# Smaller matmul forms for gates, pools and context keys in a one-core hybrid block, with weight casts moved to the last attention units

## The chip, the cores and the metric

The kernel runs on one core of a Trainium2 chip. The metric is the device time of one execution in microseconds (us). The kernel before took 1061.37 us in the median of three runs (1061.03 to 1061.40).

A core has five engines that run their own instruction streams side by side and wait for one another by semaphores: TensorE (PE in the profile; its weight loads are listed as PEld), VectorE (DVE), ScalarE (ACT), GpSimd (POOL) and SyncE (SP), which here issues most DMA transfers.

## The reference: what is computed

One layer on 1024 latent tokens (a grid of 16 rows of 64) and 256 context tokens, width 1024, all in float32:

```
mod_x = silu(c) @ w_mod + b_mod              # six rows: sh1, sc1, gt1, sh2, sc2, gt2
h_x = rmsnorm(x) * (1 + sc1) + sh1           # the context's h_c likewise, from c_ctx
u, q, k, v = h_x @ w_in                      # u is 512 wide, q, k, v are 512 wide (8 heads of 64)
attn = neighbourhood_attention(q, k, v, k_c, v_c, rpb)    # 8 x 16 window and all context keys
pool: for g, w in ((0, 2), (1, 4), (2, 8), (3, 16)):      # 128 features each
    d_g = centred_mean(u_g, w) - u_g                      # along the tokens
    y_g = d_g @ pool_w[g] * pool_scale_g
mix = concat(y, attn) @ w_out
x = x + gt1 * rmsnorm(mix)
x = x + gt2 * rmsnorm(relu(rmsnorm-modulated(x) @ w1) ** 2 @ w2)
```

Three things matter here. The context's keys are `h_c @ w_in[:, k]`, and attention needs them with features on the partitions. The gates `gt1` and `gt2` are rows of 1024 values that later multiply every token. Each pool group ends in a product with a 128 x 128 matrix.

## The kernel before, in words

**Numbers in halves.** Most products run in float32r, in three passes. An operand is split into a high part (a cast on ScalarE) and a low part (the difference, on DVE): `split`, L142, and `high_low`, L151, for weights. `three`, L167, then issues high x high, high x low and low x high as three matmuls (L168 to L170) that accumulate in one PSUM bank. A product over 1024 inputs has eight k-tiles of 128, so 24 matmuls. Three small kinds of product run in plain float32 instead: the sums of the gates (L198), the context keys' transposes (L542) and the pools' products (L603).

**Stages**, in the order in which TensorE comes to them: inputs, norms and modulation; latent keys; context keys and values; latent values; the pools' projections; the queries, with both gates and the pools' products between them; attention; the output projection; and an MLP done by a Strassen scheme.

**Context keys** (L522 to L530). Per group of 128 context tokens the tokens are stationary and the weights' 512 features move: 24 matmuls of 512 columns, and ScalarE copies the bank to `kct`. Since tokens are then on the partitions, each group is turned by four float32 transposes (`pkct`, L542) in the loop of the context values, and a second ScalarE copy puts it into `kcT`.

**Gates** (`mod_gate`, L193). A row of `w_mod`'s product is summed over k-tiles on DVE (`mod_sum`, L183) into a page `acc`, which still has 128 partial sums, one to a partition. A matmul with a matrix of ones adds the partitions and leaves the row in all of them: two float32 matmuls of 512 columns. DVE multiplies each half with the gain row `gp`. One row of the result goes to DRAM and is read back later for all partitions (`gate_page`). The sums are issued piece by piece as background work: `background` (L478) advances them and runs the closing step, the gate itself, at the next call. There are four of these rows: two column forms for the MLP's shift and scale, then gate a and gate b.

**Pools.** For each of four groups, two projections (`pu{g}_{b}`, one to a half of the tokens) are copied by ScalarE (L614) into a page `u{g}`. `pooled` (L566) makes the window sums with doubling adds on DVE, using two pages `sa{g}` and `sb{g}`, repairs the edges with small operations, and leaves the difference `d`. `pool_out` (L599) multiplies it with `pwt`, two matmuls for a group (`py{g}_{b}`), and writes the scaled result as a high part (ScalarE, L605) and a low part (DVE, L606).

**Queries** (`queries`, L650). Eight projections `pq{j}_{b}`: j is a pair of heads, b a half of the tokens. The copy that scales and reverses q runs on ScalarE (L656) into a page for each two j. All of b = 0 comes first, then `pq0_1`, the pools' products, `pq1_1`; the other two stand among the first attention units.

**Attention** (loop from L837). 32 units (four pairs of heads by eight tiles of tokens), in a software pipeline of i = 0 to 35. The loads of the output weights are issued at the units in `LOADS`, and their splits, eight halves, at the units in `HALVES` (L790): `weight_split` (L805) casts on ScalarE and leaves the difference on DVE to the next unit's `low` (L797).

**What sets the order.** Inside `in_order` blocks (L103) the engines named keep the order in which the code issues. Elsewhere a scheduler decides, from dependences and buffers. Three pools matter: 33 pages of 128 x 1024 floats (`act`, L88), four raw-weight pages (`wraw`, L86) and eight pages for split weights (`whl`, L87). In PSUM there are six banks for general use and two longer-lived ones. A page or bank is taken again only when its last reader is done, and the wait for that reader stands on the engine that writes next.

Of the kernel before, what the change touches and what calls it, by code (L numbers as in the profile page):

```python
# [17 lines left out]
P = 128  # L18
D = 1024
# [60 lines left out]
def hybrid_block(ctx, tc, x, ctx_in, w_mod, b_mod, gp1, gp2, w_in, pool_w, rpb, w_out, w1, w2, vectors,  # L80
# [17 lines left out]
    def page(name, dt=F32):  # L98
        return act.tile([P, 1024], dt, tag="pg", name=name)
# [42 lines left out]
    def split(src, hi, lo):  # L142
        nc.scalar.copy(hi, src)  # L143
        nc.vector.tensor_tensor(lo, src, hi.bitcast(F32), sub)  # L144

    def load(name, src):
        raw = wraw.tile([P, 1024], F32, tag="raw", name=f"{name}w")
        nc.sync.dma_start(raw.rearrange("p (a b) -> p a b", b=src.shape[-1]), src)
        return raw
# [13 lines left out]
    def wk(w, k, lo, c, n):  # L163
        return w[k // 2][lo][:, (k % 2) * 512 + c : (k % 2) * 512 + c + n]
# [18 lines left out]
    def mod_sum(name, c, alloc, sT):  # L183
# [4 lines left out]
        for k in range(KT):  # L188
            w = load(f"wm{name}_{k}", w_mod[k * P : (k + 1) * P, c * D : (c + 1) * D])
            nc.vector.scalar_tensor_tensor(acc, w, sT[:, k : k + 1], acc, mul, add)  # L190
            yield acc

    def mod_gate(name, acc, gp, bank):  # L193
        g = load(f"gp{name}", gp.rearrange("(o d) -> o d", o=1).to_broadcast([P, D]).rearrange("p (a b) -> p a b", a=2))
        for h in range(2):
            hs = slice(h * 512, (h + 1) * 512)
            ps = bank(f"pg{name}{h}")
            nc.tensor.matmul(ps, ones, acc[:, hs], start=True, stop=True)  # L198
            nc.vector.tensor_tensor(acc[:, hs], ps, g[:, hs], mul)

    def mod_column(name, acc, bank):
        ps = bank(f"pc{name}")
# [20 lines left out]
    with tc.tile_pool(name="ps1", bufs=6, space=PSUM) as ps1, tc.tile_pool(name="tmp1", bufs=3) as tmp:  # L223

        def bank(name):
            if name[:2] == "pm" or name in ("pxt1_0", "pxt0_2", "pxt1_7", "pct2", "pct3"):
                return lasting(name)
            return ps1.tile([P, 512], F32, tag="mm", name=name)

        def once(name, shape):  # L230
            return tmp.tile(shape, F32, tag=name, name=name, bufs=1)
# [257 lines left out]
        def mod_row(name, c, gp):  # L489
            for acc in mod_sum(name, c, page, sx):  # L490
                yield

            def close():
                mod_gate(name, acc, gp, bank)
                gates[name] = dram.tile([1, D], F32, tag=f"g{name}", name=f"g{name}")
                nc.sync.dma_start(gates[name], acc[0:1, :])

            closing.append(close)

# [14 lines left out]
        def token_group(ps, w, hk):  # L514
            for k in range(KT):
                hi, lo = hk(k)
                three(ps, hi, lo, wk(w, k, 0, 0, 512), wk(w, k, 1, 0, 512), k == 0, k == KT - 1)
# [2 lines left out]
        lat_tok = lambda b, i: lambda k: (hx[b][k][:, i * P : (i + 1) * P], hx[b][k][:, 512 + i * P : 512 + (i + 1) * P])  # L520

        kcp = page("kcT")  # L522
        kct = page("kct").rearrange("p (i f) -> p i f", i=2)
        raw_v = [load(f"wv{kk}", pair(w_in, kk, 1536, 512)) for kk in range(KT // 2)]
        for i in range(2):
            ps = bank(f"pkc{i}")
            token_group(ps, wgt, ctx_tok(i))
            if i:
                wgt = [high_low(f"wv{kk}", raw_v[kk]) for kk in range(KT // 2)]
            nc.scalar.copy(kct[:, i], ps)  # L530
        startup.close()
        with tc.issue_after(last[ET.DVE]):
            background(4)
# [1 line left out]
        for i in range(2):  # L535
            ps = bank(f"pvc{i}")
            token_group(ps, wgt, ctx_tok(i))
            nc.scalar.copy(vcp[:, i * 512 : (i + 1) * 512], ps)
            background()
            pt = bank(f"pkct{i}")  # L540
            for j in range(4):
                nc.tensor.transpose(pt[:, j * P : (j + 1) * P], kct[:, i, j * P : (j + 1) * P], ident)  # L542
            nc.scalar.copy(kcp.rearrange("p (j i t) -> p i j t", j=4, i=2)[:, i],
                               pt.rearrange("p (j t) -> p j t", j=4))
        kc = kcp.rearrange("p (j t) -> p j t", j=4)

        vp = [page(f"v{i}") for i in range(4)]
        for m in range(NM):
# [10 lines left out]

        pwt = once("pwt", [P, 4, P])  # L560
        nc.sync.dma_start(pwt, pool_w.rearrange("g c d -> c g d"))
        edg = once("edg", [P, 4, 16])
        nc.sync.dma_start(edg, edge.rearrange("o (g e) -> o g e", g=4).to_broadcast([P, 4, 16]))
        dT = []
# [32 lines left out]


        def pool_out(g):  # L599
            dv = dT[g].rearrange("p (r m c) -> p m r c", r=QR, m=NM)  # L600
            for b in range(2):
                ps = bank(f"py{g}_{b}")
                nc.tensor.matmul(ps, pwt[:, g, :], dv[:, 4 * b : 4 * b + 4], start=True, stop=True)  # L603
                mp = page(f"mix1_{g}", F32R) if b else wraw.tile([P, 1024], F32R, tag="raw", name=f"mix0_{g}")
                nc.scalar.activation(mp[:, :512], ps, AF.Identity, scale=pscol[:, g : g + 1])  # L605
                nc.vector.scalar_tensor_tensor(mp[:, 512:], ps, pscol[:, g : g + 1], mp[:, :512].bitcast(F32), mul, sub)  # L606
                mix[b][g] = mp

        for g in range(4):
            up = page(f"u{g}")  # L610
            for b in range(2):
                ps = bank(f"pu{g}_{b}")
                feature_group(ps, wgt, g * P, b, range(KT))
                nc.scalar.copy(up.rearrange("p (r m c) -> p m r c", r=QR, m=NM)[:, 4 * b : 4 * b + 4],  # L614
                                   ps.rearrange("p (m r c) -> p m r c", m=4, r=QR))
            dT.append(pooled(g, up))


        tabs, msk = [], []
# [30 lines left out]
        def queries(j, b, ps, n):  # L650
            feature_group(ps, wgt, j * P, b, range(KT))
            if j % 2 == 0:
                qp[b] = page(f"q{b}_{j}")
            qT[j][b] = qp[b][:, (j % 2) * 512 : (j % 2) * 512 + 512]
            background(n)
            nc.scalar.activation(qT[j][b].rearrange("p (m t) -> p m t", t=P)[:, :, ::-1],  # L656
                                 ps.rearrange("p (m t) -> p m t", t=P), AF.Identity, scale=-(HD ** -0.5))
# [3 lines left out]
            queries(j, 0, bank(f"pq{j}_0"), (1, 2, 3, 99)[j])  # L661
        mask_page()
        tables(0)
        queries(0, 1, bank("pq0_1"), 0)
        for g in range(4):
            pool_out(g)


    with (
# [117 lines left out]

        kks = (2, 3, 0, 1)
        raw_o, wo = {}, {}
        LOADS, HALVES = (8, 10, 17, 19), (12, 13, 14, 20, 21, 22, 28, 30)  # L790
        lows = []

        def high(src, hi, lo):
# [11 lines left out]
        def weight_split(n):  # L805
            kk, cs = kks[n // 2], slice(n % 2 * 512, n % 2 * 512 + 512)
            if n % 2 == 0:
                wo[kk] = [whl.tile([P, 1024], F32R, tag="hl", name=f"wo0_{kk}{x}") for x in "hl"]
            hi, lo = wo[kk]
            high(raw_o[0, kk][:, cs], hi[:, cs], lo[:, cs])  # L810
# [22 lines left out]
            nc.vector.tensor_tensor(mp1[t][:, hs], ps, G1[:, hs], mul)  # L833

        with in_order(ET.PE, ET.Activation, ET.DVE, ET.SP):
            queries(1, 1, bank("pq1_1"), 0)
            for i in range(N + 4):  # L837
                if i < N and units[i][1] == 2 and units[i][0] < 3:
                    tables(units[i][0] + 1)
                if i in LOADS:  # L840
                    weight_load(0, kks[LOADS.index(i)])
                if i == N - 2:
                    G1 = gate_page("a")
                if i > 3:
                    weighed(i - 4)
                low()
                if i > 8 and i % 8 == 7:
                    mixed_split(i // 8 - 1, 1)
                if i > 0 and i % 8 == 0:
                    mixed_split(i // 8 - 1, 0)  # L850
                if i in HALVES:
                    weight_split(HALVES.index(i))
                if i < N:
                    scores(i)
                else:

                    if i == N:
                        po = ps_s.tile([P, 1024], F32, tag="S", name="po")[:, :512]
                    out_sums(po, wo, 0, ((0, 1), (2, 3, 4), (5, 6, 7), ())[i - N])
                if 1 < i <= N + 1:  # L860
                    turn(i - 2)
                    fifth_kept(i - 2)
                if i < N:
                    exps(i, 0)
                if 1 < i <= N + 1:
                    turn_kept(i - 2, 0, nc.scalar.copy)
                if i < N:
                    exps(i, 1)
                if 1 < i <= N + 1:
                    turn_kept(i - 2, 1, nc.vector.tensor_copy)  # L870
                if i < 2:
                    queries(2 + i, 1, bank(f"pq{2 + i}_1"), 0)
                if 0 < i <= N:
                    share(i - 1)
                if 2 < i <= N + 2:
                    values(i - 3)
            mixed_split(3, 1)
            low()
            out_kept(0, 0, po, page("jo0_0")[:, :512])
            po = bank("po1")  # L880
            out_sums(po, wo, 1, range(8))
            out_kept(0, 1, po, page("jo0_1")[:, :512])
# [497 lines left out]
```

## Time and profile before

| | |
|---|---|
| median of three runs | 1061.37 us |
| the profiled execution's own time | 1061.53 us |
| its span, first to last instruction | 1059.7 us |
| TensorE busy | 1045.5 us, 99% |
| DVE, ScalarE, GpSimd busy | 685.6, 507.5, 55.7 us |
| the two gates' matmuls | 1.72 us each |
| the eight pools' products | 6.87 us |
| the context's eight transposes | 2 x 0.44 us |

A row of a timeline or group names start (or place), busy time, engine, line, operation, the tile written and the tiles read, and the count. "idle before <-X" tells how long the engine stood before the instructions and what ended it. In the chain each row is a stretch of work that the next one waited for, or followed on the same engine. PEclk is the TensorE clock granted, 1.00 at full speed.

### The profile page before, as it was taken

The page shows a single profiled execution, that of the slowest core. Times are in us where ns is not written, and L with a number is a line of the kernel's source. Part 1 is how long each engine was busy: PE and PEld are TensorE (multiplying, and loading weights), DVE is VectorE, ACT ScalarE, POOL GpSimd, SP SyncE. Part 2 cuts the span into 40 slices and gives each one's busy share as a digit, 9 for nine tenths or more (in the row PEclk, how much of TensorE's full clock was granted, in tenths as well). Part 3 has the DMA queues.
Part 4 walks back from the last instruction along what each step waited for, and adds up shares of the span by engine and source line. Part 5 has one row for each costly group of instructions (what it writes and reads, how often), then busy time and mean ns, then how long its engine had stood idle before and what let it go on. Part 6 is the DMA issues. An engine that isn't in the chain of part 4 may idle for free.

```text
span 1059.7 us, 15246 instructions
## 1 busy us (share of the span) xinstructions
PE 1045.5 (99%) x5870; PEld 856.4 (81%) x5870; DVE 685.6 (65%) x1071; ACT 507.5 (48%) x882; POOL 55.7 (5%) x109
## 2 busy tenths in 40 slices
PE   8999999999999999999999999999999999999996
PEld 6788888867878888888888888888888888888885
DVE  5536624846998225799987666664577666557586
ACT  7563021236998123886555454554553335334441
POOL 2020000030120003200000000000000000000001
PEclk9999999999999999999999999999999999999998
DMA  9906740531111605445745345345597666556556
GB/s 342 326 21 230 240 146 0 165 107 55 35 39 57 159 1 180 147 150 182 255 169 179 130 146 182 129 159 189 212 354 263 233 238 218 198 165 206 168 191 203
DMA packets 94268, 179.37 MB, mean 169 GB/s; under 512 B 6898, under 2 KB 39154, under 8 KB 94196
## 3 DMA queue, kind: packets, MB, share of 16 engines
q1 hardware_dynamic: 76644, 144.80, 41.6%
q10 hardware_dynamic: 16272, 29.40, 7.5%
q0 software_dynamic: 1280, 4.21, 1.1%
q8 instruction: 46, 0.75, 0.3%
q14 instruction: 26, 0.21, 0.1%
HBM read 140.62 MB, written 37.76 MB: 168 GB/s over the span
## 4 chain that ended last, share of the span: by engine, by line
PE 89%; ACT 4%; DVE 3%; issue 1%; DMA 1%; POOL 1%; SPq 0%; POOLq 0%; DVEq 0%; ACTq 0%
PE pk L400 4%; PE S L697 3%; PE pyv L170 3%; PE pyz L170 3%; PE pyx L170 3%; PE pyx L168 3%; PE phz L169 3%; PE phv L169 3%; PE phv L168 3%; PE phz L168 3%; PE pyz L169 3%; PE pyv L169 3%; PE pyv L168 3%; PE pyz L168 3%; PE phv L170 3%; PE phz L170 3%
## 5 line engine op out<-in xcount | busy, mean ns | idle before, releaser
L1029 ACT ACTIVATE c<-c 128x512 f32<-128x512 f32 x48 | 30.3, 631 | 59.9 <-DVE c L1142 23.3
L720 ACT ACTIVATE sp<-sp,nm 128x640 f32<-128x640 f32 (+1 forms) x64 | 51.4, 804 | 7.8 <-DVE nm L711 7.3
L711 DVE CUSTOM_DVE_ANT_0 sp<-S,tab 128x640 f32<-128x640 f32 (+1 forms) x56 | 42.8, 802 | 16.1 <-PE S L697 9.4
L144 DVE TENSOR_TENSOR wpS<-S,wpS 128x512 fp32r<-128x512 f32 x64 | 43.6, 686 | 11.9 <-ACT wpS L143 11.9
L170 PE MATMUL phx<-thB,wpA 128*128 128x512 f32 x128 | 49.9, 390 | 0.0
L168 PE MATMUL phx<-thB,wpA 128*128 128x512 f32 x128 | 49.9, 390 | 0.0
L169 PE MATMUL phx<-tlB,wpA 128*128 128x512 f32 x128 | 49.8, 389 | 0.0
L143 ACT CAST wpS<-S 128x512 fp32r<-128x512 f32 x64 | 39.2, 616 | 18.2 <-PE phy L170 7.8
L139 POOL TENSOR_TENSOR ry<-vy,nhalf 128x1 f32<-128x1 f32 x8 | 4.4, 550 | 600.7 <-DVE vy L137 600.7
L1030 ACT ACTIVATE c<-c 128x512 f32<-128x512 f32 x48 | 30.3, 631 | 8.1 <-DVE sa L1100 7.4
L1136 DVE TENSOR_TENSOR c<-phz,u 128x512 f32<-128x512 f32 x16 | 11.0, 690 | 32.2 <-PE phz L170 32.1
L170 PEld LDWEIGHTS phx<-thB,wpA 128*128 128x128 f32 x128 | 24.0, 188 | 5.2 <-DVE wpA L144 0.2
L697 PE MATMUL S<-kT,q 64*128 64x384 f32 (+1 forms) x128 | 27.8, 495 | 0.4 <-DVE nm L711 0.4
L168 PEld LDWEIGHTS phx<-thB,wpA 128*128 128x128 f32 x128 | 24.0, 188 | 5.0
L169 PEld LDWEIGHTS phx<-tlB,wpA 128*128 128x128 f32 x128 | 24.0, 188 | 4.9
L833 DVE TENSOR_TENSOR mp<-pw,Ga 128x512 f32<-128x512 f32 x14 | 9.6, 688 | 27.5 <-ACT jo L130 27.5
L773 PE MATMUL pa<-pt,v 128*64 128x128 f32 x352 | 25.9, 279 | 1.2 <-ACT px L753 0.6
L168 PE MATMUL phy<-thT,wpS 128*128 128x512 f32 x64 | 24.9, 389 | 0.0
L169 PE MATMUL phy<-tlT,wpS 128*128 128x512 f32 x64 | 24.9, 389 | 0.0
L170 PE MATMUL phy<-thT,wpS 128*128 128x512 f32 x64 | 24.9, 389 | 0.0
L168 PE MATMUL phz<-thT,wpS 128*128 128x512 f32 x64 | 24.9, 389 | 0.0
L169 PE MATMUL phz<-tlT,wpS 128*128 128x512 f32 x64 | 24.9, 389 | 0.0
(922 smaller groups left out, 3269.4 us busy)
## 6 DMA issues: line engine op xcount, KB each, us to landing
b<-in_w SPq DMA_DIRECT2D x64, 512.0 KB, 4.6
hrS<-hdS SPq DMA_DIRECT2D x32, 512.0 KB, 5.1
hrA<-hdA SPq DMA_DIRECT2D x24, 512.0 KB, 5.5
wm<-in_w_mod SPq DMA_DIRECT2D x16, 512.0 KB, 9.7
wa_0w<-in_w SPq DMA_DIRECT2D x16, 512.0 KB, 4.9
wa_1w<-in_w SPq DMA_DIRECT2D x16, 512.0 KB, 4.0
hdA<-c ACTq DMA_DIRECT2D x32, 256.0 KB, 2.1
hdS<-sa ACTq DMA_DIRECT2D x32, 256.0 KB, 4.4
```

The source lines that it names most:

```text
L143: nc.scalar.copy(hi, src)
L144: nc.vector.tensor_tensor(lo, src, hi.bitcast(F32), sub)
L168: nc.tensor.matmul(ps, ahi, bhi, start=first, stop=False, skip_group_check=more)
L169: nc.tensor.matmul(ps, ahi, blo, start=False, stop=False, skip_group_check=more)
L170: nc.tensor.matmul(ps, alo, bhi, start=False, stop=last, skip_group_check=more)
L400: nc.tensor.matmul(pks[b][j], wk(wgt, k, low, j * P, P), r, start=(k == 0 and n == 0), stop=(k == KT - 1 and n == 2))
L697: nc.tensor.matmul(S[e][:, c0 : c0 + keys.shape[1]], q[hs, cols], keys[hs], start=True, stop=True)
L711: nc.vector.tensor_tensor_reduce(out=to, in0=s, in1=bt, scale=1.0, scalar=BIG, op0=add, op1=ALU.min, accum_out=nm)
L720: nc.scalar.activation(sp, sp, AF.Exp, bias=least[i, e], scale=-1.0, accum_out=sums[i][:, e : e + 1])
L773: nc.tensor.matmul(pa[e * HD : (e + 1) * HD, cols], v[:, f : f + HD], turns[i][:, e, c] if c < 4 else fifths[i][:, :, (e + 1) * HD : (e + ...
L1029: nc.scalar.activation(r, src, AF.Relu)
L1030: nc.scalar.activation(r, r, AF.Square)
```

## The change

Five edits.

1. Context keys are computed with features first: the weights are stationary and the 256 context tokens move. Four groups (j, 128 features each) of 24 matmuls of 256 columns; ScalarE copies each bank straight into `kcT`. The transposes, `kct` and its copies are gone.
2. A gate's row is summed in four column groups: four float32 matmuls of 256 columns, each on 32 of the array's columns, so that quarter c of the row lies on partitions 32c to 32c + 31. One DVE operation of 128 x 256 multiplies by the gain, whose quarters come by four loads; the store takes four DMAs.
3. Pools' products run in three float32r passes. Each `d` is split into high and low by halves of the tokens, in eight more pages `d{g}_{b}`; `pool_w` is split once.
4. `background()` is called after each of the pools' projections, so sums of the gates come earlier; the products from `pq0_1` to `pq1_1` keep their order on TensorE.
5. `HALVES` puts three of the eight weight splits at i = 32, 32 and 33, one at 29, and the others as before or one unit off.

In the program as built, gate a's matmuls stand behind the first projection of pool group 1 and gate b's behind the third query; before, both stood among the queries.

```diff
     def mod_gate(name, acc, gp, bank):
-        g = load(f"gp{name}", gp.rearrange("(o d) -> o d", o=1).to_broadcast([P, D]).rearrange("p (a b) -> p a b", a=2))
-        for h in range(2):
-            hs = slice(h * 512, (h + 1) * 512)
-            ps = bank(f"pg{name}{h}")
-            nc.tensor.matmul(ps, ones, acc[:, hs], start=True, stop=True)
-            nc.vector.tensor_tensor(acc[:, hs], ps, g[:, hs], mul)
+        g = wraw.tile([P, 1024], F32, tag="raw", name=f"gp{name}w")[:, :256]
+        quarters = gp.rearrange("(c o f) -> c o f", c=4, o=1)
+        for c in range(4):
+            nc.sync.dma_start(g[32 * c : 32 * c + 32, :], quarters[c].to_broadcast([32, 256]))
+        ps = bank(f"pg{name}")
+        for c in range(4):
+            nc.tensor.matmul(ps[32 * c : 32 * c + 32, :256], ones[:, :32], acc[:, c * 256 : (c + 1) * 256],
+                             start=True, stop=True)
+        nc.vector.tensor_tensor(acc[:, :256], ps[:, :256], g, mul)
...
-                nc.sync.dma_start(gates[name], acc[0:1, :])
+                for c in range(4):
+                    nc.sync.dma_start(gates[name][:, c * 256 : (c + 1) * 256], acc[32 * c : 32 * c + 1, :256])
...
         kcp = page("kcT")
-        kct = page("kct").rearrange("p (i f) -> p i f", i=2)
+        kc = kcp.rearrange("p (j t) -> p j t", j=4)
...
-        for i in range(2):
-            ps = bank(f"pkc{i}")
-            token_group(ps, wgt, ctx_tok(i))
-            if i:
+        for j in range(4):
+            ps = bank(f"pkc{j}")[:, :CTX]
+            for k in range(KT):
+                three(ps, wk(wgt, k, 0, j * P, P), wk(wgt, k, 1, j * P, P), *hc[k], k == 0, k == KT - 1)
+            if j == 3:
                 wgt = [high_low(f"wv{kk}", raw_v[kk]) for kk in range(KT // 2)]
-            nc.scalar.copy(kct[:, i], ps)
+            nc.scalar.copy(kc[:, j], ps)
...
-            pt = bank(f"pkct{i}")
-            for j in range(4):
-                nc.tensor.transpose(pt[:, j * P : (j + 1) * P], kct[:, i, j * P : (j + 1) * P], ident)
-            nc.scalar.copy(kcp.rearrange("p (j i t) -> p i j t", j=4, i=2)[:, i],
-                               pt.rearrange("p (j t) -> p j t", j=4))
-        kc = kcp.rearrange("p (j t) -> p j t", j=4)
...
+        pwh, pwl = (tmp.tile([P, 512], F32R, tag=f"pw{n}", name=f"pw{n}", bufs=1) for n in "hl")
...
         def pool_out(g):
-            dv = dT[g].rearrange("p (r m c) -> p m r c", r=QR, m=NM)
             for b in range(2):
                 ps = bank(f"py{g}_{b}")
-                nc.tensor.matmul(ps, pwt[:, g, :], dv[:, 4 * b : 4 * b + 4], start=True, stop=True)
+                hi, lo = dT[g][b]
+                gs = slice(g * P, (g + 1) * P)
+                three(ps, pwh[:, gs], pwl[:, gs], hi, lo, True, True)
...
-                nc.scalar.copy(up.rearrange("p (r m c) -> p m r c", r=QR, m=NM)[:, 4 * b : 4 * b + 4],
-                                   ps.rearrange("p (m r c) -> p m r c", m=4, r=QR))
-            dT.append(pooled(g, up))
+                with in_order(ET.Activation) as kept:
+                    nc.scalar.copy(up.rearrange("p (r m c) -> p m r c", r=QR, m=NM)[:, 4 * b : 4 * b + 4],
+                                       ps.rearrange("p (m r c) -> p m r c", m=4, r=QR))
+                if g == 1 and b == 0:
+                    with tc.issue_after(kept[ET.Activation]):
+                        split(pwt.rearrange("p g d -> p (g d)"), pwh, pwl)
+                background()
+            dv = pooled(g, up).rearrange("p (r m c) -> p m r c", r=QR, m=NM)
+            dT.append([])
+            for b in range(2):
+                d = page(f"d{g}_{b}", F32R)
+                hi, lo = d[:, :512], d[:, 512:]
+                bands = lambda t: t.rearrange("p (m r c) -> p m r c", m=4, r=QR)
+                split(dv[:, 4 * b : 4 * b + 4], bands(hi), bands(lo))
+                dT[g].append((hi, lo))
...
-        queries(0, 1, bank("pq0_1"), 0)
-        for g in range(4):
-            pool_out(g)
+        with in_order(ET.PE) as pools:
+            queries(0, 1, bank("pq0_1"), 0)
+            for g in range(4):
+                pool_out(g)
...
-        LOADS, HALVES = (8, 10, 17, 19), (12, 13, 14, 20, 21, 22, 28, 30)
+        LOADS, HALVES = (8, 10, 17, 19), (12, 14, 20, 22, 29, 32, 32, 33)
...
-            queries(1, 1, bank("pq1_1"), 0)
+            with tc.issue_after(pools[ET.PE]):
+                queries(1, 1, bank("pq1_1"), 0)
...
-                if i in HALVES:
-                    weight_split(HALVES.index(i))
+                for n, at in enumerate(HALVES):
+                    if at == i:
+                        weight_split(n)
```

## The prediction

> **What bounds the kernel now.** I read the busy table and slices of the page first, then its shares of the chain.
>
> ```profile
> span 1059.7 us, 15246 instructions
> PE 1045.5 (99%) x5870; PEld 856.4 (81%) x5870; DVE 685.6 (65%) x1071; ACT 507.5 (48%) x882; POOL 55.7 (5%) x109
> ...
> PE   8999999999999999999999999999999999999996
> ...
> PEclk9999999999999999999999999999999999999998
> ...
> PE 89%; ACT 4%; DVE 3%; issue 1%; DMA 1%; POOL 1%; SPq 0%; POOLq 0%; DVEq 0%; ACTq 0%
> ```
>
> TensorE (PE) is busy for 99% of the span, in every slice but the ends, at full clock, and carries 89% of the chain. So each microsecond of PE work taken away shows in the span, unless the change makes PE wait. The answer is a difference of two small numbers: matmul time saved, waits added. The next rows price matmuls: three windows (start:end, length; then for PE, PEld, DVE, ACT and POOL the busy time and count; granted clock, DMA share, GB/s), groups of the chain (start, us), two timeline rows, one group of the costliest-groups list.
>
> ```profile
> 76.58:87.46 10.88, 10.88 (x49) 9.01 (x48) 4.03 (x6) 7.77 (x14) 0.00 (x0) 1.00 0.05 12
> ...
> 27.73 1.86 PE pm L351 x32
> 93.06 0.44 PE pkct L542 x4
> 98.97 0.44 PE pkct L542 x4
> 110.34 1.68 PE pcsh L204 x16
> 206.52 1.72 PE pga L198 x4
> 219.17 1.72 PE pgb L198 x4
> 220.89 6.87 PE py L603 x16
> 233.21 1.06 PE S L697 x8
> ...
> L170 PEld LDWEIGHTS phx<-thB,wpA 128*128 128x128 f32 x128 | 24.0, 188 | 5.2 <-DVE wpA L144 0.2
> ...
> 78.71 0.43 DVE L180 TENSOR_TENSOR hc<-hc7t,hc 128x256 fp32r<-128x256 f32 x1 [0.48 <-ACT hc L176]
> ```
>
> The first window holds exactly the 48 matmuls of the context keys: 10.88/48 = 0.2267 us for a float32r matmul of 512 columns. A product of three passes over eight k-tiles is 24 of them, 5.44.
>
> **The change part by part: the matmuls.**
> Pools' products: eight float32 products take 6.87 (the py group); 24 float32r matmuls take 24 x 0.2267 = 5.44. Saved 1.43; the same shape runs at this rate all around, so I see no other answer.
> Gates: the two take 1.72 each. Each becomes four matmuls of 256 columns on 32-column groups of the array. The pm group has that form: 32 records in 1.86, the eight of one gate 0.47. Saved 2 x 1.25 = 2.50. Were the column groups not to run side by side, each gate would cost what it did: 0 is the low end, and a gate of 0.43 (half a float32 pass of 512) the high one, 2.58.
> Context transposes: 2 x 0.44 = 0.88 saved, with two ScalarE copies.
> Context keys: 48 matmuls of 512 become 96 of 256, the same columns. At the same rate per column they cost 0.113, 10.88 in all; the smallest record, 0.105 in pcsh (1.68/16), is below that. No row shows a stream of 256-column matmuls with a weight load each. Upper end: the load sets the pace with its recorded 0.188: 18.05, that is 7.2 more. I take 0.12, nearer the lower end, since in the window a load record stands beside every 512-column matmul and costs nothing: 11.52, lost 0.64.
> Sum of the matmuls: -1.43 - 2.50 - 0.88 + 0.64 = -4.17.
>
> What a 256-column stream costs is what the Trainium skill speaks against. Its page "TensorE: Matmul & The Clock Gate", Part 3, "What overlaps and what doesn't", says a weight load overlaps matmuls in flight only when its row group differs, and gives P/1.2 ns for a load, 107 ns for 128. By that rule 96 loads and matmuls in series would be an estimated 96 x 0.214 = 20.5, and the kernel about 1071.5. In the window above, 48 loads with records of 9.01 us lie beside 48 matmuls inside 10.88: this trace contradicts the serial reading at 512 columns, and is silent at 256.
>
> **The waits that it adds.** The order of instructions in the changed program gives them. There are 33 activation pages (the pool `act`). The pools now hold eight more (`d{g}_{b}`), so pages of pool group 2 (`sb2`) and the first page of q come free only when the fourth query's third matmul has read its last hx page. Group 2's and 3's DVE chains and the q copies therefore slide behind the queries. The prices:
>
> ```profile
> 181.23 1.23 DVE L576 TENSOR_TENSOR sb<-sa 128x1021 f32<-128x1021 f32 x1
> ...
> 184.88 0.15 DVE L592 TENSOR_TENSOR sb<-ed,u 128x4 f32<-128x4 f32 x1
> 192.24 1.22 DVE L576 TENSOR_TENSOR sa<-u 128x1023 f32<-128x1023 f32 x1
> 193.44 1.28 DVE L190 SCALAR_TENSOR_TENSOR acca<-wma_7w,sx,acca 128x1024 f32<-128x1024 f32 x1
> 194.63 1.22 DVE L576 TENSOR_TENSOR sb<-sa 128x1021 f32<-128x1021 f32 x1
> ...
> 200.30 0.17 DVE L595 TENSOR_TENSOR sa<-ed,u 128x7 f32<-128x7 f32 x1
> ...
> 185.93 1.05 ACT L143 CAST wq0h<-wq0w 128x1024 fp32r<-128x1024 f32 x1 [0.50 <-PE pu L169]
> ...
> L614 ACT COPY u<-pu 128x512 f32<-128x512 f32 x8 | 4.7, 586 | 33.3 <-PE pu L170 33.3
> L656 ACT ACTIVATE q<-pq 128x512 f32<-128x512 f32 x6 | 3.6, 599 | 30.0 <-PE pq L170 21.8 <-DVE ed L587 8.2
> L606 DVE SCALAR_TENSOR_TENSOR mix<-py,cols,mix 128x512 fp32r<-128x512 f32 x8 | 5.7, 746 | 0.6 <-ACT mix L605 0.5
> ```
>
> I count from t = 0, where PE ends the second gate (now behind the third query).
> (1) The fourth query needs the PSUM bank that DVE frees with the gate's product: 0.2 for the matmul to land, 0.43 for the 128x256 operation, two hand-overs of 0.06: 0.75. It runs from 0.75 to 6.19.
> (2) Its third matmul ends at 1.4 and has landed at 1.7, which frees `sb2`. Three long DVE operations (181.23 to 184.88: 3.65) end at 5.35; ScalarE then does two casts of group 2 (0.53 each, half of the 1.05) and the copy of u3's first half (0.59): 7.1. `pq0_1` needs that copy's bank and starts at 7.15: a wait of 1.0. It ends at 12.59, `py0_0` at 13.27.
> (3) The second half of u3 is copied at 7.65; then DVE does group 3's chain, from 192.24 to 200.47 less one accumulation between (193.44 to 194.63): 7.0, to 14.7. Behind it on DVE stands the low part of `mix0_0`, 0.75, whose bank `py0_1` needs: PE starts at 15.45, a wait of 2.2, and ends at 16.13.
> (4) ScalarE casts group 3 (to 17.05) before its first q copy (0.60); `py1_0` needs that bank, starts at 17.7: a wait of 1.55. The other six products follow, 4.08.
> Sum of the waits: 0.75 + 1.0 + 2.2 + 1.55 = 5.5. The steps are made of operations with rows; the hand-overs and order of small DVE operations leave some 1.0 either way, 4.5 to 6.5.
>
> **What moves without PE.** These rows, in turn: the relative-position pages and their tables, a weight load by DMA, and the first score products before and after a stretch of four units, with and without weight casts.
>
> ```profile
> 219.69 4.92 POOL L641 TENSOR_TENSOR tab<-msk,U 128x128 f32<-128x128 f32 x12 [6.96 <-DMA U<-in_rpb]
> ...
> wq1w<-in_w_in SPq DMA_DIRECT2D x1, 512.0 KB, 6.3
> ...
> 252.79 0.92 PE L697 MATMUL S<-kT,q 64*128 64x384 f32 x4
> ...
> 262.53 0.70 PE L697 MATMUL S<-kcT,q 64*128 64x256 f32 x4
> ...
> 303.17 0.94 PE L697 MATMUL S<-kT,q 64*128 64x384 f32 x4
> ...
> 313.27 0.70 PE L697 MATMUL S<-kcT,q 64*128 64x256 f32 x4
> ```
>
> Tables: SP now issues the loads of U behind a wait for `py0_1`, t = 16.4; 6.96 to land and 4.92 for twelve GpSimd operations end them at 28.2. The first scores start at 27.3 (17.7 + 4.08 + 5.44) and DVE reads a table past 28.4; another query of 5.44 stands between the first units and covers it. Cost 0; without that cover at most 1.
> SP: three more loads and three more stores for each gate, with `wq`'s four loads behind the first gate's. By my estimate they are issued some 20 us ahead of their casts (185.93 and later), and a load takes 6.3: over 10 us of cover. Cost 0; each microsecond beyond that cover would delay the queries by as much.
> ScalarE and DVE: eight splits and `pwt`'s more, 9 x 0.53 and 9 x 0.69. ScalarE idles 33.3 us ahead of the u copies, and DVE's part lies beside queries; where it does not, it is in the waits above. The accumulations moved ahead into the pools' loop fall on DVE while PE has 8 x 5.44 = 43 us of projections. Cost 0.
> Weight casts: eight splits, three of them now in the last units. Four units take 9.74 without a cast (252.79 to 262.53), and 10.10 with three (303.17 to 313.27): 0.1 for a split. Three leave units where they cost this, and one joins such a stretch: -0.2 (-1.0 to +0.3).
>
> Net: -4.17 + 5.5 - 0.2 = +1.1. The profiled execution took 1061.53 (1.8 outside the span, unchanged), so 1062.6; it lies 0.16 above the median of the runs, 1061.37: **1062.5**.
>
> **The rivals.**
> Slower, by the weight loads: if loads don't hide behind 256 columns, the context keys take 0.188 a matmul, 6.5 more than taken: 1069.0. For it: the load record (0.188) is longer than 256 columns last (0.113). Against it: records of loads overlap, and their count in the window says nothing of a limit. It decides from a period of 0.130 on, where the 96 cost 1.0 more.
>
> ```profile
> 9.00:12.00 3.00, 2.05 (x16) 1.51 (x15) 2.00 (x5) 2.68 (x5) 2.33 (x3) 1.00 1.04 415
> ...
> 1048.00:1052.00 4.00, 3.63 (x17) 2.66 (x15) 1.61 (x2) 0.00 (x0) 0.55 (x1) 1.00 0.37 103
> 1052.00:1056.00 4.00, 0.00 (x0) 0.00 (x0) 2.63 (x5) 0.72 (x2) 0.55 (x1) 0.80 0.27 84
> ```
>
> Slower, by the clock: around `py0_1` PE works 0.68 of 4.4 us. If that halves the clock for the six products behind, their 4.08 takes 8.16: 1062.5 + 4.1 = 1066.6. Against it: with PE busy 2.05 of 3 us (9 to 12) the clock was 1.00, and it fell to 0.80 only in a window with no matmul at all. The Trainium skill's page "TensorE: Matmul & The Clock Gate", "HAM oscillation", has the clock halve again when waits cross the monitor's window; this trace shows such a fall for an idle stretch of 4 us, and none for one of 2.2, my longest.
> Slower, because the gates' column groups don't run side by side, so that this part doesn't do what it says: 1062.5 + 2.5 = 1065.0. The pm group speaks against it.
> Faster, without the waits: if pages come free earlier than I read, or DVE keeps up, only the matmuls count: 1061.37 - 4.17 - 0.2 = 1057.0. For it: PE waits almost nowhere in this profile. Against it: the order and page chain are fixed in the program. At half the waits it is 1059.8, within what can be told apart.
>
> **How the numbers follow.** A difference of 0.2%, 2.1 us, is about what a measurement tells from none: 1059.25 to 1063.5 counts as the same. My forecast gets 0.63, with its own range of 1060.5 to 1064.5 (0.02 faster, 0.40 same, 0.21 slower); the weight loads 0.11, the clock 0.06 and the gates 0.03, all slower; no waits 0.13, faster; other causes 0.04 (0.02 faster, 0.02 same). Together 0.17, 0.42, 0.41. The range, 1058.0 to 1067.0, leaves out the far ends: full weight loads and the case without waits.
>
> **What the profile after would show.** The window of the context keys lasts 11.5, not 10.9 or 18. Each gate takes 0.47, one product of the pools 0.68. PE idles four times between the second gate and the second batch's queries, 0.75, 1.0, 2.2 and 1.55, with DVE, ScalarE, DVE and ScalarE as releasers. The first scores start at 233.21 - 4.17 + 5.5 = 234.5, and what follows takes as long as before within 0.5. I am wrong if PE's gaps sum to less than 3 or more than 8, or the clock dips there.

## The result and the profile after

The changed kernel takes 1064.37 us in the median of eight runs (1062.81 to 1066.11), the kernel before 1061.28 (1061.03 to 1062.42). The ratio is 1.0028, 95% interval 1.0017 to 1.0039: slower by 0.28%, some 3 us. The prediction was 1062.5 with a range of 1058.0 to 1067.0. The time lies in the range, 1.9 above the forecast, and on the slower side: by the prediction's own mark, under which 1059.25 to 1063.5 counts as the same, it is slower, to which I had given 0.41, and 0.42 to "same".

The page of the changed kernel, profiled in an execution with a span of 1062.6 us:

```profile
span 1062.6 us, 15399 instructions
...
PE 1044.5 (98%) x5926; PEld 859.1 (81%) x5926; DVE 687.3 (65%) x1078; ACT 510.0 (48%) x891; POOL 55.6 (5%) x109
...
PE   8999999989999999999999999999999999999997
```

TensorE's busy time fell by only 1.0 us, and a digit 8 has appeared in the ninth slice, 212 to 239 us. That slice holds the queries and the pools' products. The waits of TensorE there, by line, releaser and time (total, times, longest); the same view of the kernel before has no row in this stretch:

```profile
PE py L168 <- DVE mix L608: 1.6, 1, 1.6
PE py L168 <- ACT q L670: 1.0, 1, 1.0
PE pq L168 <- ACT u L617: 0.8, 1, 0.8
PE pq L168 <- DVE accb L203: 0.5, 1, 0.5
```

These are the four waits of the prediction, longest first, with the releasers it named. The profile counts a gap from a matmul's modelled end; counted from the regular pace of 0.2267 us they are 0.5, 1.0, 1.8 and 1.2 (the last product before the third wait is issued at 221.06 and the next at 223.07: 2.01 less 0.23). The chain of waits shows what stood in each:

```profile
207.33 0.61 PE pgb L201 x8
207.97 0.44 DVE accb L203
208.45 0.50 PE pq L168
208.95 0.24 PE pq L169
209.19 0.25 PE pq L170
209.46 1.22 DVE sb L577
210.76 1.20 DVE sa L577
211.98 1.22 DVE sb L590
213.35 1.14 ACT d L143 x2
214.50 0.49 ACT u L617
215.03 0.50 PE pq L168
...
222.26 0.75 DVE mix L608
223.55 0.37 issue
223.92 0.61 ACT d L143
224.53 0.50 ACT q L670
225.08 0.79 PE py L168
```

Read it from the top: the gate's product on DVE holds the bank that the fourth query needs; group 2's chain on DVE starts only after that query's third matmul (209.19), and behind it come two casts and the copy of u, which `pq0_1` waits for; the low part of the first product's result (mix, 222.26) stands on DVE behind group 3's chain, and the second product waits for it; and the first q copy stands behind the casts of group 3, which the third product waits for.

One thing was not in my likeliest case. Windows over the end of this stretch, in the changed kernel (start:end, length, busy time of PE, PEld, DVE, ACT and POOL, granted clock, DMA share, GB/s), beside the context keys' window:

```profile
76.67:88.25 11.58, 11.58 (x98) 11.55 (x96) 2.27 (x4) 7.08 (x15) 0.00 (x0) 1.00 0.00 0
220.00:223.00 3.00, 1.44 (x7) 0.86 (x5) 2.85 (x11) 0.69 (x1) 0.62 (x2) 1.00 0.00 0
223.00:225.00 2.00, 0.98 (x3) 0.48 (x3) 1.44 (x8) 1.61 (x4) 0.31 (x1) 0.92 0.00 0
225.00:228.00 3.00, 2.92 (x7) 2.34 (x8) 0.85 (x2) 2.72 (x7) 0.00 (x0) 0.50 0.64 164
228.00:231.00 3.00, 3.00 (x15) 2.48 (x14) 2.68 (x5) 3.00 (x6) 2.83 (x7) 0.99 0.03 9
```

The third and fourth wait have 0.7 us of work between them. Near the end of the fourth the clock of TensorE falls to 0.50. By the shares of the windows (0.92 over 2 us, 0.50 over 3, 0.99 over 3) it does so from 224.7 to 228.1, for 3.4 us. In the window from 225 to 228 7 matmuls have run where 13 do at full clock, and the six products behind the last wait take 5.6 us (225.08 to 230.68) where they need 4.1. The first scores start at 236.28, against 233.21 before: 3.07 later, which is the whole difference of the spans (1062.6 - 1059.7 = 2.9).

### The profile page after: what moved, and what is told of

It is laid out like the page before. It is cut to its first block, busy times and chain, and to the rows that moved or that the text cites. A ratio compares the mean times of both kernels' runs of the same rounds, so it can differ in the third digit from the quotient of the medians.

```text
span 1062.6 us, 15399 instructions
## 1 busy us (share of the span) xinstructions
PE 1044.5 (98%) x5926; PEld 859.1 (81%) x5926; DVE 687.3 (65%) x1078; ACT 510.0 (48%) x891; POOL 55.6 (5%) x109
## 4 chain that ended last, share of the span: by engine, by line
PE 89%; ACT 4%; DVE 3%; issue 1%; POOL 1%; DMA 1%; SPq 0%; POOLq 0%; DVEq 0%; ACTq 0%
PE pk L404 4%; PE S L712 3%; PE pa L788 3%; PE pyv L169 3%; PE pyz L169 3%; PE pyx L170 3%; PE pyx L169 3%; PE phz L168 3%; PE phv L168 3%; PE phv L170 3%; PE phz L170 3%; PE pyz L168 3%; PE pyv L168 3%; PE pyv L170 3%; PE pyz L170 3%; PE phz L169 3%
```

## The experiments

Each kernel was timed beside the kernel before on the same chip; a ratio is to that.

**Filling the waits.** Is the low clock an effect of the idle time? Spare matmuls with no use were put where TensorE waits, so that it waits as long but is not idle.

```diff
+        spare = lasting("spare")
         with in_order(ET.PE) as pools:
...
                 three(ps, pwh[:, gs], pwl[:, gs], hi, lo, True, True)
+                if g == 0:
+                    for n in range((7, 4)[b]):
+                        nc.tensor.matmul(spare, pwh[:, gs], hi, start=True, stop=True)
```

> The changed kernel with eleven spare float32r matmuls of 512 columns into an unused PSUM bank, seven behind py0_0 and four behind py0_1, where PE waits 1.8 and 1.2 us; they change no result and no wait. Theory (the waits cool the clock): the granted clock stays 1.00 behind py1_0, the six products there take 4.1 instead of 5.6 us, the two waits stay, and the time falls by 1.5 to 1062.9, with less spread between runs. Rival (the clock fall has nothing to do with the idle time): the products still take 5.6 and the time stays 1064.4.

Measured: 1063.19 (1062.94 to 1063.63), ratio 1.0019, interval 1.0010 to 1.0027. The windows of this kernel:

```profile
220.00:223.00 3.00, 3.00 (x14) 2.17 (x12) 2.82 (x11) 0.69 (x1) 0.31 (x1) 1.00 0.00 0
223.00:225.00 2.00, 1.92 (x8) 1.24 (x7) 1.44 (x8) 1.62 (x4) 0.62 (x2) 1.00 0.00 0
225.00:228.00 3.00, 2.93 (x13) 2.42 (x14) 1.08 (x2) 3.00 (x8) 0.00 (x0) 1.00 0.41 89
```

PE reaches the products at the same moment, 225.07, but runs 13 matmuls in the window instead of 7, at 1.00. The fall of the clock follows from the idle time, and costs 1.2 us of the median. It also goes with most of the spread: of the changed kernel's eight runs the two with a mean clock of 0.998 took 1062.81 and 1062.95, and those at 0.995 took 1065.68 and 1066.11; the eleven runs with the spare matmuls lie within 0.7.

**Filling one wait.** The same with the spare matmuls at one place only, `range((7, 0)[b])` and `range((0, 4)[b])`.

> The changed kernel with spare matmuls behind py0_0 alone, so that of the two long waits only the second, 1.2 us, leaves PE idle. If the clock falls by the idle time summed over a few us (2.7 of the 3.4 us before the fall in the changed kernel), it stays at 1.00 and the time is that of both fillers, 1063.2. If one wait of about 1.2 is enough, it falls: 1064.4.

> The changed kernel with spare matmuls behind py0_1 alone, so that the first long wait, 1.8 us, is left idle and the second, 1.2 us, is filled. With the first filled instead (fill_first) the clock stayed at 1.00. If only the two waits together (2.7 us idle within 3.4) halve the clock, it stays at 1.00 here too: 1063.2. If one wait of 1.8 us is enough, it falls here: 1064.4, with the spread of the changed kernel.

Measured: 1063.13 (1062.83 to 1063.31, ratio 1.0018, interval 1.0009 to 1.0027) and 1062.71 (ratio 1.0017, interval 1.0007 to 1.0027). One window of the first, where the wait of 1.2 is left idle, and three of the second, where that of 1.8 is:

```profile
225.00:228.00 3.00, 2.97 (x13) 2.48 (x14) 1.04 (x2) 3.00 (x7) 0.08 (x1) 1.00 0.61 167
...
220.00:223.00 3.00, 1.38 (x7) 0.84 (x6) 2.85 (x12) 0.69 (x1) 0.62 (x2) 1.00 0.00 0
223.00:225.00 2.00, 1.89 (x8) 1.22 (x9) 1.43 (x5) 1.80 (x4) 0.31 (x1) 1.00 0.00 0
225.00:228.00 3.00, 3.00 (x14) 2.47 (x15) 0.93 (x3) 3.00 (x7) 0.00 (x0) 1.00 0.48 100
```

In both traces the clock stays at 1.00 with one wait alone, and the medians are those of the kernel with both filled. It takes both waits here: by 224.7, where the clock falls, TensorE has been idle for 1.8 and 0.8 us, with one product between. One of the twelve runs of the last kernel took 1068.78, with a mean clock of 0.948 against 0.997 to 0.999 in the other eleven; there is no trace of it, and I can't explain it.

**Two more pages.** Are the waits the fault of the 33 pages, as I had read, or of too much work for DVE and ScalarE? Two d pages of group 1 get a place of their own; no operation is added or removed.

```diff
-                d = page(f"d{g}_{b}", F32R)
+                d = tmp.tile([P, 1024], F32R, tag="d", name=f"d{g}_{b}", bufs=2) if g == 1 else page(f"d{g}_{b}", F32R)
```

> The changed kernel with pool group 1's two d pages taken from a pool of their own, so that 35 pages serve where 33 did; no operation is added or removed. Theory (the shortage of pages makes group 2 and 3 and the q copies late): the four waits of PE (0.5, 1.0, 1.8, 1.2 us) and the slow clock behind them (1.5) go, 6 us in all: 1058.3, 0.3% under the kernel before. Rival (DVE and ScalarE have too much to do in this stage whatever the pages): the two long waits stay, and with them the clock: 1063 or more.

Measured: 1057.95 (1057.77 to 1058.13), ratio 0.9970, interval 0.9958 to 0.9981. Its windows of the same stage:

```profile
206.00:216.00 10.00, 10.00 (x50) 7.71 (x49) 6.70 (x9) 2.07 (x5) 1.19 (x4) 1.00 0.17 49
216.00:222.00 6.00, 6.00 (x28) 4.94 (x27) 1.58 (x3) 3.91 (x8) 4.28 (x11) 1.00 0.25 70
222.00:225.00 3.00, 3.00 (x15) 2.45 (x14) 3.00 (x5) 2.95 (x5) 0.66 (x2) 1.00 0.01 3
```

PE is busy throughout, with as many instructions on DVE and ScalarE as in the changed kernel (1078 and 891). The second gate stands where it stood (207.30 against 207.33), but the query behind it does not wait. In its chain the scores start here:

```profile
229.91 1.06 PE S L712 x8
```

That is 6.4 before the changed kernel's 236.28. So the shortage of pages made all four waits and, with them, the fall of the clock. Against the kernels with spare matmuls (1063.19 and 1063.13) the waits themselves are worth 5.2.

**Without the three passes.** The pools' products in float32 again, all else changed:

```diff
-                three(ps, pwh[:, gs], pwl[:, gs], hi, lo, True, True)
+                nc.tensor.matmul(ps, pwt[:, g, :], dv[:, 4 * b : 4 * b + 4], start=True, stop=True)
...
-                d = page(f"d{g}_{b}", F32R)
-                hi, lo = d[:, :512], d[:, 512:]
...
-                split(dv[:, 4 * b : 4 * b + 4], bands(hi), bands(lo))
```

> The changed kernel with the pools' products in float32 as before, without the splits of d and of the pool weights and their pages; gates, context keys, background order and weight casts stay changed. Theory (the splits and their pages make the waits): no waits of PE between the second gate and the first scores, clock 1.00; what is left is two gates at 1.0 saved each, 0.1 from the context and 0.2 from the casts: 1061.3 - 2.3 = 1059.0. Rival (the gate's place or the accumulations moved ahead make the waits): waits stay, and 1.4 for the slower products comes on top: 1065.8.

Measured: 1059.62, ratio 0.9987, interval 0.9978 to 0.9996. The waits are gone:

```profile
206.00:216.00 10.00, 10.00 (x50) 7.68 (x50) 0.42 (x1) 1.20 (x2) 1.27 (x5) 1.00 0.32 90
...
222.00:225.00 3.00, 3.00 (x8) 1.33 (x7) 2.52 (x5) 2.32 (x5) 0.00 (x0) 1.00 0.00 0
```

So it was the splits and their pages, and neither the gates' place nor the accumulations moved ahead. Beside two_pages it also prices the passes where they have room: 1059.62 - 1057.95 = 1.7 saved.

**A query group ahead of the products.** Other work to fill the long waits:

```diff
             queries(0, 1, bank("pq0_1"), 0)
+            queries(1, 1, lasting("pq1_1"), 0)
             for g in range(4):
                 pool_out(g)
...
-            with tc.issue_after(pools[ET.PE]):
-                queries(1, 1, bank("pq1_1"), 0)
```

> The changed kernel with the query group pq1_1 moved ahead of the pools' products. Theory: the 5.4 us of the group cover the waits of 1.8 and 1.2 and keep the clock at 1.00, 4.6 saved; but the first scores now stand right behind the last product and wait some 2 us for DVE's low parts: about 1061.8. Rival (a pure shift, the uncovered wait ahead of the scores is as long as those removed and the clock falls there instead): 1064 or more.

Measured: 1063.94 (1063.68 to 1068.04), ratio 1.0032, interval 1.0020 to 1.0043: the rival's time. Its windows ahead of and behind the first scores:

```profile
232.00:234.00 2.00, 0.00 (x0) 0.00 (x0) 2.00 (x4) 0.75 (x2) 2.00 (x6) 1.00 0.72 180
234.00:236.00 2.00, 1.93 (x10) 1.36 (x11) 0.68 (x3) 0.00 (x0) 2.00 (x6) 0.83 0.23 74
236.00:238.00 2.00, 2.00 (x6) 1.61 (x5) 0.71 (x4) 1.52 (x4) 2.00 (x6) 0.50 0.04 8
```

The chain names what the scores waited for: seven low parts of the mix on DVE.

```profile
229.31 4.71 DVE mix L608 x7
234.07 1.13 PE S L713 x8
```

I had the new wait nearly right (some 2 us expected, 2.4 measured), but my theory kept the clock at 1.00, and one wait of 2.4 is enough to halve it. It fell in another place, with other work behind it.

**The gates alone**, on the kernel before (the `mod_gate` and the store of the diff, and the guard that keeps `pq1_1` behind the products).

> The kernel before with the new gates alone (four column groups, quarter loads and stores), and the order of TensorE from pq0_1 to pq1_1 held as it was. In the trace of the changed kernel a gate takes 0.78 from the start of its matmuls to the regular pace behind, against 1.77 before. Theory: 1.0 saved for each: 1061.3 - 2.0 = 1059.3. Rival (the prediction's 0.47 a gate, 2.5 in all): 1058.8. Second rival (the product's shorter way makes no difference because the group waits for its accumulations): 1061.3.

Measured: 1059.85, against 1061.14 beside it; ratio 0.9989, interval 0.9980 to 0.9998. The profiled execution is 1.9 shorter (a span of 1057.8), the medians differ by 1.3. In its chain the gates read:

```profile
206.56 0.57 PE pga L200 x8
218.74 0.64 PE pgb L200 x8
```

So a gate takes 0.6, not 1.72, and not the 0.47 of the pm group; TensorE stands idle for 0.49 before the second one. The 2.0 us that this run was expected to save (1059.3) lie just inside the interval; the prediction's 2.5 (1058.8) and no effect lie outside.

**The context keys alone**, on the kernel before.

> The kernel before with the new context keys alone. By the changed kernel's trace the keys take 11.58 instead of 10.88 and the stretch with the two transposes 11.07 instead of 11.71, so that little is left: 1061.2. Rival (the prediction's 0.24 saved): 1061.0. Rival (loads of weights that do not hide, felt elsewhere): 1062 or more.

Measured: 1061.21 against 1061.14, ratio 1.0001, interval 0.9992 to 1.0010. No difference can be told. The stretch behind the keys, from the context's values to the first of the latent values, holds the two transposes in the kernel before (first row) and not in the changed one:

```profile
87.46:99.17 11.71, 11.71 (x58) 9.71 (x56) 9.49 (x8) 2.75 (x5) 0.00 (x0) 1.00 0.92 325
...
88.25:99.32 11.07, 11.07 (x51) 9.01 (x49) 8.77 (x8) 2.67 (x4) 1.44 (x2) 1.00 0.84 285
```

It is 0.64 shorter, and the keys ahead of it are 0.70 longer (11.58 against 10.88).

**The weight casts**, alone on the kernel before, and undone in two_pages (the edit that undoes them):

```diff
-        LOADS, HALVES = (8, 10, 17, 19), (12, 14, 20, 22, 29, 32, 32, 33)
+        LOADS, HALVES = (8, 10, 17, 19), (12, 13, 14, 20, 21, 22, 28, 30)
```

> The kernel before with the weight casts alone at their new units (12, 14, 20, 22, 29, 32, 32, 33). In the traces of two_pages and two_pages_halves the stretch from the first scores to the output projection is 125.28 with the new units and 124.65 with the old, so the new ones should cost here 0.5: 1061.8. The prediction had them save 0.2: 1061.1.

> The kernel of two_pages with the weight casts at their old units (12, 13, 14, 20, 21, 22, 28, 30). If moving three of them behind the last units saves 0.2, this is 1058.15; if it saves nothing, 1057.95; if casts cost more than 0.1 each among the units, 1058.5 or more.

Measured: alone 1061.78 (1061.57 to 1061.97) against 1061.31 (ratio 1.0003, interval 0.9994 to 1.0011); undone 1057.41 (1057.33 to 1057.49), ratio 0.9965, interval 0.9952 to 0.9977. Both point to some 0.5 lost by the new units (0.5 and, each against the kernel before beside it, 0.4), though the intervals don't exclude none. The chain of two_pages shows where, at the last units:

```profile
339.14 0.52 ACT wo_0h L809
339.66 0.52 ACT wo_1h L809
340.18 0.23 ACT px L768
```

The turned rows (px) that TensorE needs next stand behind two weight casts on ScalarE. With the old units ScalarE is idle for 0.66 ahead of that copy, in the timeline of two_pages_halves:

```profile
339.67 0.32 ACT L768 COPY px<-pa 128x192 f32<-128x192 f32 x1 [0.66 <-PE pz L754]
```

From the last scores (i = 31) to the output projection's second group the new units take 0.7 longer in both pairs of traces (here 334.46 to 355.12, 20.66, against 334.45 to 354.40, 19.95). The units ahead are 0.1 shorter in this pair and 0.5 in the other; of those 0.5, 0.3 lie at i = 7, ahead of the first cast, so that the casts can have saved 0.2 there. two_pages_halves is the fastest kernel of this study: 3.7 us, 0.35%, under the kernel before.

## Why the prediction was right or wrong

**What bounds the kernel**: right. What TensorE lost in the stage of the pools showed in the span: two_pages reaches the first scores 6.4 earlier than the changed kernel, and its span is 6.5 shorter.

**Pools' products**: right. 1.43 forecast, 1.7 measured between the medians of two kernels.

**Gates**: mechanism right, size too large. I took the rate of the pm group, whose column groups are part of a longer stream. One gate is 0.6, and TensorE needs some 0.1 on either side to come back to its pace. 2.50 forecast; 1.9 in the trace and 1.3 between the medians.

**Context keys and transposes**: the window of 11.58 is the 11.5 that I forecast, and the rival of weight loads that don't hide is out: 96 loads fill 11.55 of 11.58 us of the window, and a 256-column matmul still passes each 0.12. Whether the loads are what keeps it from 0.113, no run tells. The rule that I weighed from the Trainium skill's page "TensorE: Matmul & The Clock Gate", Part 3, "What overlaps and what doesn't" (a load overlaps matmuls in flight only when the row group differs), is not what this stream shows: its loads and matmuls both fill the same 11.58 us. What failed is the other half: the transposes were worth 0.64, not 0.88. With that the whole edit is worth nothing, as ctx_alone shows.

**The waits**: right in cause, place and releasers, and nearly in size: 0.75, 1.0, 2.2 and 1.55 forecast, 0.5, 1.0, 1.8 and 1.2 in the trace; 5.5 in sum forecast, 5.2 between the fillers and two_pages, where the first matmul behind each wait adds about 0.1. The first scores were forecast at 234.5 and came at 236.28; by the traces the difference, 1.7, is some 1.5 for the clock, 0.6 for the gates and 0.3 for the context keys, less 0.6 by which the waits were shorter than forecast. The rival without waits, 1057.0, comes near two_pages (1057.95).

**The clock**: this is where the prediction went wrong most, and by its own sign: it was to be wrong if "the clock dips there", and it did. The forecast put this term at nothing; as a rival it had 0.06, because PE had been busy 2.05 of 3 us elsewhere at full clock and no single wait came near the idle stretch of 4 us that the trace shows at the end. That trace could not rule it out: TensorE's longest wait in it is 1.6 us, and between that and the idle end it has no stretch to judge by. The waits add up: 1.8 and 1.2 with one product between them act together. The rival named the place and the work that it would slow, but its price was too high, 4.1, since the fall lasts 3.4 us, some 3 of them while products run, and not over all six products: 1.5 in the profile, 1.2 in the median.

**Weight casts**: -0.2 forecast, about +0.5 by the medians, whose intervals don't exclude none. The gain among the units is there in the traces (0.1 and 0.2); the step that failed is "Three leave units where they cost this", with nothing set against them at the end. In the last units ScalarE carries what TensorE waits for, too.

**The sum** with the measured terms: waits and clock 6.4 (1064.37 - 1057.95), and all the rest -3.3 (1057.95 - 1061.28): +3.1. Against my +1.1, 0.7 comes from the casts, 0.9 from the clock and the waits (1.2 - 0.3), and what is left, 0.4, would be the gates and the context less the larger gain of the passes. Taken one by one these come to 0.6 with the gates' 1.9 and to 1.2 with their 1.3, so the parts add up only within some 0.8. That the time still lies in the range, and just inside the 1060.5 to 1064.5 that the forecast took for its own, is owed to their width: the sum gave about a third of the slowdown, with two terms, the clock and the casts, put too low.

What stays open: the attention units i = 5 to 7 are 0.4 us shorter than in the kernel before in the changed kernel, gates_alone, no_passes, two_pages and two_pages_halves, and not in ctx_alone. The gates alone don't settle it: with both waits filled they are 0.2 shorter, and in halves_alone, with the old gates, 0.3. I didn't try why.

## What to carry to other kernels

Where TensorE is the bound, a cheaper matmul form that needs more buffers can cost more than it saves: look for the first buffer that the pool can't give, follow what its late release delays on the other engines, and count the waits that come of it. Two pages more, from a pool of their own, turned 0.28% slower into 0.30% faster. And add up idle times of TensorE that lie near each other before you rule out that its clock will fall.

## What I had not expected of the hardware

Waits of 1.8 and 1.2 us with 0.7 us of work between them halved the granted clock for 3.4 us, while in the traces with either of them alone it stayed at 1.00. One wait of 2.4 us did it as well, with the fall 1.3 us after work had begun again at 234.07 and the clock back at full before 239. The clock does not seem to have fallen in every run of the changed kernel: two of eight kept the mean clock of the kernel before, 0.998. The Trainium skill's page "TensorE: Matmul & The Clock Gate", "HAM oscillation", names waits that cross the monitor's window; in the changed kernel no single wait did it, but idle time of 2.6 us in the 3.4 us from 221.3 to 224.7, with work in between. Over how long a stretch idle time counts, no run here shows.
